# Hybrid decoder layer: a third raw weight tile, a fourth place for split weights, a stock of 72 working tiles, later loads for the per-layer embedding, and queries of heads 0 and 1 built without transfers

## The chip, the cores and the metric

One core of a Trainium2 chip runs the kernel. The metric is device time in microseconds for one execution; the median of three runs is compared. A profile is one further execution, and its times count from its first instruction.

## The reference

One layer over 512 tokens of width 1024, in float32:

```python
h = rmsnorm(x, attn_norm);  proj = h @ w_in
mq, mk, mv, rq, rk, rv, rg = split(proj)          # seven parts of 512 columns
moba = block-sparse attention(mq, mk, mv)          # 8 heads of 64, blocks of 256 keys, ALiBi
ret  = groupnorm(retention(rq, rk, rv)) * silu(rg) # 4 heads of 128, chunks of 256
x = x + concat(moba, ret) @ w_out
h = rmsnorm(x, ffn_norm);  u = causal_dwconv3(h @ w_up)
x = x + (gelu(u) * (h @ w_gate)) @ w_down          # 2816 wide
g = sigmoid(rmsnorm(x, ple_norm) @ w_ple_gate)
x = x + (p @ w_ple) * g                            # per-layer embedding, 256 inputs
out = rmsnorm(x, final_norm)
```

With 512 tokens there are two blocks of 256 keys and three may be chosen, so every allowed block is taken: the attention is plain causal attention with ALiBi.

## The kernel before

**Three products for one.** TensorE multiplies in a reduced float32 format. Each operand is therefore split: a high part, which ScalarE (ACT) rounds, and a low part, the rest, which VectorE (DVE) or GpSimd (POOL) subtracts. `mm3` (L91) issues high x high, high x low and low x high, each with 512 columns.

**Weights.** `fetch` (L127) loads a job of weights, up to 1 MB, from the SP queue into a raw tile `wr`; there are two. `prepare` (L139) splits part after part into pairs of `wh` and `wl` tiles; there are three places for each. A pair holds the 8 slices that one projected tile needs. A place is free again when TensorE has done the last product that reads it. `need` (L158) asks for one part more than the caller uses next. In the attention phase POOL does the subtraction for `wl`, elsewhere DVE does.

**The stock.** All other working tiles, [128, 512] float32 each, come from one pool, `heap`, of `HEAP` = 80 tiles, through `h2k` (L60). A tile goes back when its last reader is done. What needs a tile waits for one.

**Order.** TensorE's order is the program order; a loop at the end (L833) ties each of its instructions to the one before. For the other engines and the queues a planner of the framework writes the order at compile time, with its own costs: an engine takes the earliest instruction of the program that it thinks ready. On the chip each engine then follows its list, and an instruction that waits holds up all behind it.

**The start.** `enter(k)` (L269) transposes block k of x into PSUM (four transposes, `xt`), scales it by the norm's gain `gv` and splits it into h1. The gain comes as rows, `grow`, by a transfer from POOL's queue, and is transposed (L221) ahead of the first `xt`.

**Attention.** `project` (L354) makes one tile of 128 output rows by 512 tokens: 24 matmuls, then DVE scales the PSUM tile into `pt` (L361) and it is split. For `mq` and `mk` the two heads of a tile are brought apart by transfers within the chip's memory: for head e of the pair, one tile holds the high part of its queries in 64 partitions and the low part in the other 64 (L369 to L371), so that one matmul takes both; `mk` gives four tiles, and 8 transfers, in the same manner.

After four retention heads (loop at L609, the last turn of which projects `mk` 0, `mq` 0 and `mk` 1) the MoBA loop (L634) runs i = 0 to 9, two turns for a pair of heads: `moba_scores` (L457) for block i % 2 of pair i // 2, in two steps; `moba_values` of two turns earlier; `moba_turn` (transposes of the probabilities) of the turn before. Between these stand fillers: the other projections `mq` 1 to `mq` 3 in i = 0 to 4, `out_first` (products with the second half of w_out) from i = 1, `ple_product` from i = 5, whose first one needs `ple_weights(0, 0)`, `ple_weights(0, 1)` and both of `ple_turn`.

`softmax` (L446): DVE adds the ALiBi bias and takes the minimum (L449), ACT takes the exponential (L452), DVE the reciprocal (L454) and the scaling (L455). `moba_bias` (L442) makes a head's bias tile on POOL. `ple_load` (L560) brings 1.5 MB from SP's queue into six tiles of the stock; `ple_weights` (L577) turns one of them into a high (ACT) and a low part (POOL); `ple_turn` (L570) transposes p on TensorE and splits it.

After this come the convolutional FFN (two halves of 12 and 10 tiles of 128) and the gate of the embedding with the final norm.

Of the kernel before, what the change touches and what calls it, by code (L numbers as in the profile page):

```python
# [31 lines left out]
RMS_EPS = 1e-6  # L32
GN_EPS = 1e-5
NEG = -3.0e38
HEAP = 80


V_FFN, V_PLE, V_RET, V_CW, V_CB, V_ROWS = 0, 8, 16, 20, 86, 108
# [3 lines left out]
def hybrid_layer_kernel(ctx, tc, x, p, attn_norm, w_in, ret_norm, w_out, ffn_norm, w_up, w_gate,  # L42
# [13 lines left out]
    def nm(s):  # L56
        n_of[s] = n_of.get(s, 0) + 1
        return f"{s}_{n_of[s]}"
# [5 lines left out]
    def ps(s):  # L64
        return psum.tile([P, T], F32, tag="ps", name=nm(s))
# [4 lines left out]
    def f(a):  # L70
        return a.bitcast(F32)
# [55 lines left out]
    def fetch(upto):  # L127
        while issued[0] < min(upto, len(jobs)):
            load, (nk, cols, _), _ = job = jobs[issued[0]]
            raw = wpool.tile([P, 2048], F32, tag="wr", name=nm("wr"), bufs=2)[:, :nk * cols]  # L130
            raw = raw.rearrange("p (k c) -> p k c", k=nk)
            load(raw)
            job[2] = raw
            issued[0] += 1
# [4 lines left out]
    def prepare(upto):  # L139
        while halved[0] < min(upto, len(parts)):  # L140
            key, j, i, heaped = parts[halved[0]]
            final = halved[0] + 1 == len(parts) or parts[halved[0] + 1][1] != j
            fetch(j + 2 if final else j + 1)
            (nk, cols, per), raw = jobs[j][1:]
            if heaped:
                ready[key] = split(raw[:, i, :], "wg")
            else:
                part = raw[:, :, i * per:(i + 1) * per] if per else raw[:, 2 * i:2 * i + 2, :]
                n, c = part.shape[1:]
                hi, lo = (wpool.tile([P, 1024], F32R, tag=tag, name=nm(tag), bufs=3)[:, :n * c].rearrange(  # L150
                    "p (k c) -> p k c", k=n) for tag in ("wh", "wl"))
                nc.scalar.activation(hi, part, AF.Copy)  # L152
                aside = key[0] in ("mv", "rq", "rk", "rg", "mq", "mk", "out") and key not in (("mv", 0), ("mv", 1))
                (nc.gpsimd if aside else nc.vector).tensor_tensor(lo, part, f(hi), op=ALU.subtract)  # L154
                ready[key] = (hi, lo)
            halved[0] += 1
# [35 lines left out]
    make_identity(nc, ident)  # L192
    xn, vraw = [], []
    grow = const.tile([ND, P], F32, name="grow")
    nc.gpsimd.dma_start(grow, attn_norm[0].rearrange("(r c) -> r c", c=P))
    for k in range(ND):
        t = h2k("xn")
        nc.sync.dma_start(t.rearrange("p (t c) -> p t c", t=NT),
# [18 lines left out]
    nc.sync.dma_start(vrow[V_CW:V_CB, :], conv_w[0].rearrange("j (r c) -> (j r) c", c=P))  # L217
    nc.sync.dma_start(vrow[V_CB:V_ROWS, :], conv_b[0].rearrange("(r c) -> r c", c=P))
    fetch(2)
    gv_ps = ps("gv")  # L220
    nc.tensor.transpose(gv_ps[:, :ND], grow, ident[:ND, :ND])  # L221
    gv = const.tile([P, ND], F32, name="gv")
# [44 lines left out]
    ss = const.tile([P, ND, NT], F32, name="ss")  # L267

    def enter(k):  # L269
        tp = ps("xt")  # L270
        for t in range(NT):
            nc.tensor.transpose(tp[:, t * P:(t + 1) * P], xn[k][:, t * P:(t + 1) * P], ident)
        wh = hi_of(vraw[k], "rvw")
        g = gv[:, k:k + 1]
        hi = hi_of(tp, "h1", scale=g)
        r = h2k("xT")
        nc.scalar.activation(r, tp, AF.Copy)
        xT.append(r)
        wl, lo = h2k("rvwl", F32R), h2k("h1l", F32R)
        nc.vector.tensor_tensor(wl, vraw[k], f(wh), op=ALU.subtract)  # L280
        nc.vector.scalar_tensor_tensor(lo, tp, g, f(hi), op0=ALU.mult, op1=ALU.subtract)
        h1.append((hi, lo))
        return wh, wl
# [70 lines left out]
    def project(name, i):  # L354

        w = need((name, i))
        acc = ps("pj")
        for k in range(ND):
            mm3(acc, (w[0][:, k, :], w[1][:, k, :]), h1[k], k == 0, k == ND - 1)
        t = h2k("pt")  # L360
        nc.vector.scalar_tensor_tensor(t, acc, DH ** -0.5 if name == "mq" else 1.0, r1b, op0=ALU.mult, op1=ALU.mult)  # L361
        if name == "rg":
            sil[i] = h2k("sil")
            nc.scalar.activation(sil[i], t, AF.Silu)
        elif name == "mq":

            both = split(t, "mq")
            two = [h2k("mq2", F32R) for _ in range(2)]
            for e in range(2):  # L369
                for part, half in zip(both, HALF):  # L370
                    nc.sync.dma_start(f(two[e][half]), f(part[HALF[e]]))  # L371
            qs[name, i] = two
        elif name == "mk":

            both = split(t, "mk")
            two = [[h2k("mk2", F32R) for _ in range(2)] for _ in range(2)]
            for part, tiles in zip(both, two):
                for e in range(2):
                    for half in HALF:
                        nc.sync.dma_start(f(tiles[e][half]), f(part[HALF[e]]))  # L380
            qs[name, i] = two
        else:
            qs[name, i] = split(t, name)
# [225 lines left out]
    for h in range(HR):  # L609
# [7 lines left out]
        project(*tiles[3 * h + 1])  # L617
        ret_sums(h)
        project(*tiles[3 * h + 2])
    for h in range(2):  # L620
        moba_bias(h)
    ple_load()

    big = [lambda n=n, h=h: project(n, h) for n, h in feature_tiles[15:]]
    mid = [lambda dt=dt: out_first(dt) for dt in range(ND)]
# [8 lines left out]
    for i in range(HM + 2):  # L634
# [11 lines left out]
        for e in range(2):  # L646
            if 1 <= i <= HM:
                moba_turn((i - 1) // 2, (i - 1) % 2, e)
            for go in fills[3 * i + 1 + e]:
                go()  # L650
        if 1 <= i < 5:
            ple_weights((i - 1) // 2, (i - 1) % 2)
        if i in (2, 3):
            ple_turn(i - 2)
    out_accs[2] = out_two(2, range(3))
    for dt in range(0, 4, 2):
        out_two(dt, [3], out_accs[dt])
# [216 lines left out]
```

## Time and profile before

| what | value |
|---|---|
| runs of before, us | 702.09, 702.34, 704.38; median 702.34 |
| profiled execution, us | 704.48 |
| its span, first to last instruction, us | 702.60 |
| mean granted clock of TensorE | 0.995 of full speed |
| busy: PE, DVE, ACT, POOL, us | 685.4, 433.5, 282.7, 125.4 |
| moved, mean rate | 71.91 MB, 102 GB/s |

The span leaves out what lies around the instructions (1.88 us in the profiled execution). PE's busy time is a union of overlapping matmuls, so that its complement is what TensorE stood still.

### The profile page before, as it was taken

To read this page: it belongs to the slowest core of one execution; us is meant where nothing else is said; L and a number is where in the kernel's file an instruction comes from. 1 tells how busy PE (TensorE), PEld (TensorE's weight loads), DVE (VectorE), ACT (ScalarE), POOL (GpSimd) and SP (SyncE) were. 2 spreads that over 40 slices of the span, in tenths; PEclk is the share of its full clock that TensorE was granted. 3 is DMA by queue.
4 is the path that set the end of the run, shared out by engine and by line. 5 is a ranking of instruction groups with operands and counts; after the bars stand their busy time and mean duration, and the time that the engine had idled before them with its cause. 6 is when DMAs were issued, how large, how long until landed. Compare 5 with 4: busy or idle time off the path is not lost.

```text
span 702.6 us, 8467 instructions
## 1 busy us (share of the span) xinstructions
PE 685.4 (98%) x3200; PEld 569.5 (81%) x3200; DVE 433.5 (62%) x784; ACT 282.7 (40%) x459; POOL 125.4 (18%) x100
## 2 busy tenths in 40 slices
PE   9999999998899999999999999999999999999995
PEld 6888888886777888888888888888888888888884
DVE  5675677764577875876556653224565565466497
ACT  5534543333565773553334331122343343354311
POOL 6135242325355211000000000000000000000145
PEclk9999999999999999999999999999999999999999
DMA  8335224338554201233233122233332321345003
GB/s 265 116 103 150 61 76 115 81 91 216 144 169 125 68 2 60 63 118 119 81 100 119 47 88 90 94 121 110 109 115 66 119 67 48 133 137 185 1 1 119
DMA packets 73726, 71.91 MB, mean 102 GB/s; under 512 B 2530, under 2 KB 62806, under 8 KB 73686
## 3 DMA queue, kind: packets, MB, share of 16 engines
q1 hardware_dynamic: 73510, 71.11, 33.4%
q8 instruction: 25, 0.41, 0.2%
q10 hardware_dynamic: 144, 0.26, 0.1%
q14 instruction: 15, 0.12, 0.0%
q0 software_dynamic: 32, 0.00, 0.0%
HBM read 62.97 MB, written 2.10 MB: 93 GB/s over the span
## 4 chain that ended last, share of the span: by engine, by line
PE 89%; DVE 6%; ACT 2%; DMA 2%; issue 1%; POOL 0%; SPq 0%; DVEq 0%; ACTq 0%
PE gate L93 6%; PE gate L95 6%; PE dn L95 6%; PE up L95 6%; PE up L93 6%; PE dn L93 6%; PE gate L94 6%; PE dn L94 6%; PE up L94 6%; PE pj L93 5%; PE pj L94 5%; PE pj L95 4%; PE ou L93 2%; PE ou L94 2%; PE ou L95 2%
## 5 line engine op out<-in xcount | busy, mean ns | idle before, releaser
L152 ACT ACTIVATE wh<-wr 128x1024 fp32r<-128x1024 f32 (+2 forms) x108 | 105.3, 979 | 214.9 <-PE dn L94 66.4
L154 DVE TENSOR_TENSOR wl<-wr,wh 128x1024 fp32r<-128x1024 f32 (+2 forms) x78 | 84.6, 1085 | 44.7 <-ACT wh L152 44.6
L154 POOL TENSOR_TENSOR wl<-wr,wh 128x1024 fp32r<-128x1024 f32 x30 | 73.0, 2432 | 153.9 <-ACT wh L152 152.9
L93 PE MATMUL gate<-h2h,wh 128*128 128x512 f32 x176 | 68.7, 390 | 0.0
L95 PE MATMUL gate<-h2h,wl 128*128 128x512 f32 x176 | 68.5, 389 | 0.0
L94 PE MATMUL gate<-h2l,wh 128*128 128x512 f32 x176 | 68.5, 389 | 0.0
L93 PE MATMUL up<-h2h,wh 128*128 128x512 f32 x176 | 68.5, 389 | 0.0
L94 PE MATMUL up<-h2l,wh 128*128 128x512 f32 x176 | 68.5, 389 | 0.0
L95 PE MATMUL up<-h2h,wl 128*128 128x512 f32 x176 | 68.5, 389 | 0.0
L93 PE MATMUL dn<-ach,wh 128*128 128x512 f32 x176 | 68.5, 389 | 0.0
L94 PE MATMUL dn<-acl,wh 128*128 128x512 f32 x176 | 68.5, 389 | 0.0
L95 PE MATMUL dn<-ach,wl 128*128 128x512 f32 x176 | 68.5, 389 | 0.0
L93 PE MATMUL pj<-h1h,wh 128*128 128x512 f32 x160 | 64.1, 401 | 1.2 <-DVE corner L504 1.1
L95 PE MATMUL pj<-h1h,wl 128*128 128x512 f32 x160 | 63.1, 394 | 0.0
L94 PE MATMUL pj<-h1l,wh 128*128 128x512 f32 x160 | 62.9, 393 | 0.0
L700 POOL MEMSET u<- 128x2 f32 x22 | 2.3, 102 | 290.6 <-DVE c L707 290.6
L711 DVE TENSOR_TENSOR ga<-gate,r2b 128x512 f32<-128x512 f32 x22 | 15.2, 691 | 41.4 <-PE gate L95 41.4
L701 DVE TENSOR_TENSOR u<-up,r2b 128x512 f32<-128x512 f32 x22 | 15.1, 692 | 39.3 <-PE up L95 39.3
L94 PEld LDWEIGHTS dn<-acl,wh 128*128 128x128 f32 x176 | 33.0, 188 | 6.9
L95 PEld LDWEIGHTS gate<-h2h,wl 128*128 128x128 f32 x176 | 33.0, 188 | 6.9
L94 PEld LDWEIGHTS up<-h2l,wh 128*128 128x128 f32 x176 | 33.0, 188 | 6.9
L94 PEld LDWEIGHTS gate<-h2l,wh 128*128 128x128 f32 x176 | 33.0, 188 | 6.9
(233 smaller groups left out, 1415.8 us busy)
## 6 DMA issues: line engine op xcount, KB each, us to landing
wr<-in_w_up_dram SPq DMA_DIRECT2D x11, 1024.0 KB, 5.4
wr<-in_w_gate_dram SPq DMA_DIRECT2D x11, 1024.0 KB, 5.4
wr<-in_w_in_dram SPq DMA_DIRECT2D x20, 512.0 KB, 3.9
wr<-in_w_down_dram SPq DMA_DIRECT2D x8, 768.0 KB, 4.2
wr<-in_w_down_dram SPq DMA_DIRECT2D x8, 640.0 KB, 4.1
wr<-in_w_ple_gate_dram SPq DMA_DIRECT2D x4, 1024.0 KB, 5.1
wr<-in_w_out_dram SPq DMA_DIRECT2D x3, 1024.0 KB, 5.2
xn<-in_x_dram SPq DMA_DIRECT2D x8, 256.0 KB, 5.9
```

The costliest lines, as they stand in the source:

```text
L93: nc.tensor.matmul(acc, a[0], b[0], start=first, stop=False)
L94: nc.tensor.matmul(acc, a[0], b[1], start=False, stop=False)
L95: nc.tensor.matmul(acc, a[1], b[0], start=False, stop=last)
L152: nc.scalar.activation(hi, part, AF.Copy)
L154: (nc.gpsimd if aside else nc.vector).tensor_tensor(lo, part, f(hi), op=ALU.subtract)
L700: nc.gpsimd.memset(u[:, 0:2], 0.0)
L701: nc.vector.tensor_tensor(u[:, 2:], up, r2b, op=ALU.mult)
L711: nc.vector.tensor_tensor(ga, gate, r2b, op=ALU.mult)
```

## The change

Six edits, in the order of the diff: the stock goes from 80 tiles (of 2 KB in each partition) to 72, which gives 16 KB. A third raw tile takes 8 KB, and a fourth place for `wh` and `wl` takes 4 KB each. `grow` is loaded from ACT's queue in place of POOL's, and the first four transposes `xt` stand ahead of that of `gv`. For pair 0 ACT rounds each head's half of the queries straight into the half of the tile where the high part stands, and DVE writes the rest into the other half: two ACT and two DVE instructions on 64 partitions, in place of one and one on 128 and four transfers. The bias of heads 0 and 1 is made in turn 1 of the retention loop. `ple_load` goes from ahead of the MoBA loop to the end of turn 1, `ple_weights` from turns 1 to 4 to turns 3 to 6, `ple_turn` from turns 2 and 3 to turns 3 and 4.

```diff
-HEAP = 80
+HEAP = 72
@@ fetch
-            raw = wpool.tile([P, 2048], F32, tag="wr", name=nm("wr"), bufs=2)[:, :nk * cols]
+            raw = wpool.tile([P, 2048], F32, tag="wr", name=nm("wr"), bufs=3)[:, :nk * cols]
@@ prepare
-                hi, lo = (wpool.tile([P, 1024], F32R, tag=tag, name=nm(tag), bufs=3)[:, :n * c].rearrange(
+                hi, lo = (wpool.tile([P, 1024], F32R, tag=tag, name=nm(tag), bufs=4)[:, :n * c].rearrange(
@@ start
-    nc.gpsimd.dma_start(grow, attn_norm[0].rearrange("(r c) -> r c", c=P))
+    nc.scalar.dma_start(grow, attn_norm[0].rearrange("(r c) -> r c", c=P))
...
+    def turned(k):
+        tp = ps("xt")
+        for t in range(NT):
+            nc.tensor.transpose(tp[:, t * P:(t + 1) * P], xn[k][:, t * P:(t + 1) * P], ident)
+        return tp
+
+    turned_first = turned(0)
     gv_ps = ps("gv")
@@ enter
-        tp = ps("xt")
-        for t in range(NT):
-            nc.tensor.transpose(tp[:, t * P:(t + 1) * P], xn[k][:, t * P:(t + 1) * P], ident)
+        tp = turned(k) if k else turned_first
@@ project, name == "mq"
-            both = split(t, "mq")
             two = [h2k("mq2", F32R) for _ in range(2)]
+            if i == 0:
+                for e in range(2):
+                    nc.scalar.activation(two[e][HALF[e]], t[HALF[e]], AF.Copy)
+                    nc.vector.tensor_tensor(two[e][HALF[1 - e]], t[HALF[e]], f(two[e][HALF[e]]), op=ALU.subtract)
+            both = split(t, "mq") if i else ()
@@ retention loop, then MoBA loop
-    for h in range(2):
-        moba_bias(h)
-    ple_load()
+        if h == 1:
+            for e in range(2):
+                moba_bias(e)
...
-        if 1 <= i < 5:
-            ple_weights((i - 1) // 2, (i - 1) % 2)
-        if i in (2, 3):
-            ple_turn(i - 2)
+        if i == 1:
+            ple_load()
+        if 3 <= i < 7:
+            ple_weights((i - 3) // 2, (i - 3) % 2)
+        if i in (3, 4):
+            ple_turn(i - 3)
```

## Rows read from the trace of the kernel before

**Rows 1.** Windows: length, busy us (count) of five engines, clock, DMA share, GB/s

```profile
150.00:175.00 25.00, 22.15 (x101) 18.11 (x100) 11.17 (x31) 8.26 (x13) 11.99 (x6) 0.93 0.71 190
175.00:200.00 25.00, 22.43 (x115) 18.19 (x114) 17.24 (x52) 13.20 (x33) 13.46 (x7) 1.00 0.67 172
200.00:225.00 25.00, 24.44 (x135) 20.85 (x134) 18.27 (x52) 15.77 (x36) 11.21 (x7) 1.00 0.37 103
...
300.00:400.00 100.00, 100.00 (x444) 82.80 (x444) 62.13 (x81) 40.48 (x50) 1.00 (x10) 1.00 0.32 99
...
650.00:702.60 52.60, 43.92 (x235) 37.16 (x234) 36.86 (x93) 10.67 (x17) 20.09 (x13) 0.97 0.11 41
```

**Rows 2.** Waits of PE: line, released by; us in total, times, longest

```profile
PE ms L470 <- DMA mq<-mql: 2.7, 1, 2.7
...
PE ms L470 <- DVE mkl L82: 1.2, 1, 1.2
PE pj L93 <- DVE corner L504: 1.1, 2, 0.8
PE ou L93 <- DVE ml L449: 0.7, 2, 0.4
PE pw L93 <- DVE corner L504: 0.7, 1, 0.7
```

**Rows 3.** Timeline of PE, 158 to 167: start, duration, what, idle before and releaser

```profile
161.86 0.39 PE L470 MATMUL ms<-mk,mq 128*128 128x256 f32 x1 [2.68 <-DMA mq<-mql]
...
163.33 0.63 PE L95 MATMUL pj<-h1h,wl 128*128 128x512 f32 x1
...
166.74 0.40 PE L94 MATMUL pj<-h1l,wh 128*128 128x512 f32 x1
```

**Rows 4.** Timeline of DVE, 153 to 173

```profile
153.81 2.40 DVE L233 TENSOR_SCALAR rrs<-rrv 128x4 int32<-128x4 int32 x1
...
156.93 0.68 DVE L361 SCALAR_TENSOR_TENSOR pt<-pj,r1b 128x512 f32<-128x512 f32 x1
...
158.31 0.69 DVE L82 TENSOR_TENSOR mql<-pt,mqh 128x512 fp32r<-128x512 f32 x1
...
161.16 1.92 DVE L82 TENSOR_TENSOR mkl<-pt,mkh 128x512 fp32r<-128x512 f32 x1 [0.70 <-ACT mkh L75]
...
172.86 0.16 DVE L454 RECIPROCAL mi<-mt 128x1 f32<-128x1 f32 x1 [8.09 <-ACT me L452]
```

**Rows 5.** Timeline of ACT, 157 to 190

```profile
157.64 0.63 ACT L75 ACTIVATE mqh<-pt 128x512 fp32r<-128x512 f32 x1 [3.41 <-DVE pt L361]
...
169.96 1.06 ACT L152 ACTIVATE wh<-wr 128x1024 fp32r<-128x1024 f32 x1 [8.84 <-PE pj L94]
...
189.16 1.06 ACT L152 ACTIVATE wh<-wr 128x1024 fp32r<-128x1024 f32 x1 [4.47 <-issue]
```

**Rows 6.** Timeline of POOL, 153 to 231

```profile
153.79 2.40 POOL L154 TENSOR_TENSOR wl<-wr,wh 128x1024 fp32r<-128x1024 f32 x1 [5.33 <-ACT wh L152]
160.18 2.36 POOL L154 TENSOR_TENSOR wl<-wr,wh 128x1024 fp32r<-128x1024 f32 x1 [3.99 <-ACT wh L152]
...
229.67 1.29 POOL L581 TENSOR_TENSOR wpl<-wpr,wph 128x512 fp32r<-128x512 f32 x1 [3.09 <-ACT wph L75]
```

**Rows 7.** Timeline of SP's queue, 166 to 169: issues

```profile
166.45 1.98 SPq L564 DMA_DIRECT2D wpr<-in_w_ple_dram  x4
```

**Rows 8.** Chain that ended last, in order of time: start, us, what

```profile
177.45 5.76 DMA mq<-mql
```

**Rows 9.** Timeline of PE, 227 to 229

```profile
228.04 0.40 PE L93 MATMUL pw<-wph,pTh 128*128 128x512 f32 x1
```

**Rows 10.** Timeline of PE and its weight loads, 4 to 8

```profile
4.59 0.24 PE L221 MATMUL gv<-ident,grow 8*128 8x8 f32 x1 [0.19 <-POOL sq L287]
4.76 2.21 PE L272 MATMUL xt<-ident,xn 128*128 128x128 f32 x8
...
7.92 0.29 PEld L95 LDWEIGHTS rv<-rvwh,h1l 128*128 128x128 f32 x1 [0.77 <-DVE h1l L281]
```

## The prediction

> **What bounds the kernel now.** I read the windows first. TensorE (PE) is busy 685.4 of 702.60 us, and from 250 to 650 us it never stands: 444 matmuls in 100 us, 0.225 us apart, are its own pace [rows 1]. Nothing in this change takes a matmul away, so only what PE stands still, or runs slowly, can be won. It stands 17.2 us in all. In 650 to 702.60 it is 8.7 us, nearly all of it after its last matmul, where the last tiles are normed and written; no edit touches that. At the start it is 1.7 us. The rest, 6.7 us, lies in 150 to 250, the MoBA stage: 2.85 and 2.57 us in its first two quarters, then about 0.6 in each of the others [rows 1].
>
> The waits of PE name these: 2.7 us until the last transfer of queries 0 has landed, 1.2 us in the same place for pair 1 (put down to DVE, but it is again the transfer, below), and 2.5 us in five waits for DVE to empty a PSUM tile (1.1, 0.7 and 0.7) [rows 2]. The timeline adds a cost that is no wait: after the 2.68 us the matmuls run 0.43 us apart from 163.33 to 166.74, where 8 take 3.41 us in place of 8 x 0.225 = 1.8. The granted clock of the quarter is 0.93 [rows 1, 3]: 1.6 us are lost to the lower level. The two pairs of ACT and DVE rows show why DVE is late. An ACT instruction that splits a weight part waits 8.84 us for PE to free a place, and the first exponential stands behind it; DVE waits 8.09 us for that exponential. The same happens at 189.16, with 4.47 us [rows 4, 5].
>
> **The change, part by part.** *Queries of heads 0 and 1.* Now `pt` ends at 157.61, ACT rounds until 158.27, DVE subtracts until 159.00, the four transfers follow and PE starts at 161.86, 2.68 us after it ran out of work at 159.18 [rows 3 to 5]. After: ACT rounds head 0's half (at most the 0.63 of the full tile) until 158.27, DVE writes its rest (at most 0.69) until 159.00; head 1's pair follows on ACT until 158.9 and on DVE until 159.7. The trace shows no subtraction that writes into other partitions than it reads; for its cost I take that of the same shape on 128, 0.69, which also is the upper end, and nothing for the lower, since the later head matters only from 159.4, when head 0's two matmuls are over. PE then waits about 0.3 to 0.5 us for head 1. Gain 2.7 - 0.5 = 2.2 us (0.5 to 2.7). A stop of 1.2 us did not lower the clock in 175 to 200 [rows 1, 2], so the 1.6 us return too. The bias made in the retention loop costs POOL the same two instructions earlier, where DVE and PE wait for none of them, and takes POOL out of the way to the first minimum.
>
> *Pair 1.* Its last transfer is issued at 177.45 and takes 5.76 us, behind 1.5 MB of `ple_load`, issued from 166.45 on, and a weight load [rows 7, 8]. Its `pt` itself is late, since DVE is held by the exponential. Both go: the load moves behind turn 1, and the exponential no longer stands behind the weight split, since with a fourth place that split waits for the end of the projection before, 159.0 in place of 169.96. Gain 1.2 us (0 to 1.2).
>
> *Fourth place, third raw tile.* A raw tile more lets a load start a job earlier; in the stretches where PE is full that is worth nothing, and its cover is PE's own 0.225 us pace. In the MoBA stage the fourth place moves 13.3 us of blocked ACT time (8.84 and 4.47) off the softmax [rows 5]. Of the 2.5 us that PE waits for DVE I take half, 1.3 us (0 to 2.5): DVE is the nearest thing to a second bound there, 18.27 us of 25 [rows 1], and part of its lateness is its own.
>
> *Start.* The four transposes `xt` now run at 4.76, behind that of `gv`, which waits for `grow` [rows 10]; in the new order they need block 0 of x alone, and `gv` follows. What this can shorten is the 0.77 us that the weight load at 7.92 stands for the low part of block 0 [rows 10]. The other four transposes of that row wait for the next block of x and don't move, so that PE gets there no earlier. Gain 0.3 us (0 to 0.8). The load on ACT's queue costs ACT an issue while ACT has nothing to do.
>
> *What may be given back.* `ple_weights(0, 1)` moves to turn 4, the place of the present `ple_weights(1, 1)`, whose POOL part ends at 229.67 + 1.29 = 230.96. The first filler that needs it does so at 228.04 [rows 6, 9]. Were engines as late as now, PE would wait 2.9 us; with DVE and ACT less behind I take 0.7 us (0 to 2.9). SP's queue issues the six `ple` loads ahead of turn 2's, and whatever waits there for a tile of the stock waits with them: the transfers of `mk` 2 and `mq` 2, which PE reads in turn 4 only.
>
> *Stock of 72.* I counted, in the order of the program, the tiles whose last reader is still to come. Before, the count is 78 in turn 1, 80 in turn 2 and at most 88 in turn 3, where `mk` 3 is split, against 80. Of these 6, 7 to 10 and 10 belong to the embedding; with its loads later they are 0, 6 and 6, so that the change needs 72, 78 and 84, against 72. The overdraft is 0, 6 and 12 where it was 0, 0 and 8. So some tiles of turns 2 and 3 are handed out late; with eight PSUM tiles between PE and DVE I count nothing for it in the likeliest case, and the rival below prices it.
>
> The sum against the profiled execution: 2.2 + 1.6 + 1.2 + 1.3 + 0.3 - 0.7 = 5.9 us, so its 704.48 would be 698.6. The median of the runs is 702.34, 2.1 below the profiled one; I set the forecast against it: **696.4 us**.
>
> **Rivals.** *The new subtraction is held by POOL.* A POOL split of 2.40 us begins at 153.79, and a four-column DVE instruction beside it takes 2.40 us; the one of 160.18 stretches DVE's `mkl` from 0.69 to 1.92 [rows 4, 6]. If the fourth place moves such a split onto 158.3 to 159.7, head 0's rest ends up to 2.4 us late, PE stops as long as now, and the clock falls as now: 2.2 + 1.6 are lost, 700.2 us. The Trainium skill (SBUF — State Buffer, section Who interferes with whom) has the rule: a VectorE instruction with two inputs in SBUF and a GpSimd instruction that reads SBUF exclude each other for the whole instruction, and the one issued first wins; the two rows agree with it, and by it the two new subtractions, both with two such inputs, are exposed. Against it: POOL is idle from 156.19 to 160.18, and its splits follow the ends of PE's projections, which don't move.
>
> *The weight split still stands ahead of the exponential.* With four places ACT's next split waits for the end of the next projection, and the planner may again list it first. Then DVE's waits stay and pair 1 is late in `pt`, though not in transfers: 2.2 + 1.6 + 0.3 - 0.7 = 3.4, 698.9 us. For it: both blocked splits follow that pattern. Against it: the bias is ready earlier, and so is the exponential.
>
> *What PE wins, it waits for later.* DVE is busy 17.24 of 25 and 18.27 of 25 us in 175 to 225 [rows 1]. If its chain sets the stage's end, PE arrives earlier at the same wait, and about 701.5 us are left. Against it: DVE itself stands 8.09 us in one piece.
>
> *The stock starves (slower).* Place: turn 3, where 84 tiles are asked of 72. If what is held back is the destination of a minimum, its two PSUM tiles stay full, the softmax of block 1 starts only when `moba_values` frees four tiles, and PE reaches the transposes of turn 4 before it. The nearest row for a softmax held back is DVE's 8.09 us [rows 4]; with the clock's 1.6 that is 9.7 us against 6.6 won without it, 705 us. It decides from 6.6 us of standing. For it: the overdraft grows by half. Against it: with 8 too many, before, PE waited only 0.3 us in that turn, the shorter of the two waits for `corner` [rows 2].
>
> **How the numbers follow.** Likeliest 0.56, its own range 693.5 to 699; POOL's hold 0.08; the split still first 0.13; waits later 0.10; starved stock 0.13. With every gain at its upper end (2.7 + 1.6 + 1.2 + 2.5 + 0.8 = 8.8) the time is 693.5. The range 693.4 to 702.4 leaves out the starved stock and a little below. Within 0.3% (2.1 us) a measurement of this kernel can't tell a change from none. Faster: the likeliest, the split, and half of POOL's hold with some of the waits: 0.75. Same: 0.12. Slower: 0.13.
>
> **What would show it.** In the changed profile the first `ms` should follow the projection of `mk` 1 within 0.5 us and no matmul after it be 0.43 apart; ACT's exponentials of pair 0 should come at 160 to 163, not 171; `ms` of pair 1 should wait for nothing; `rv` at 7.92 should move up; the first `pw` shows in its wait whether the late `ple_weights` is in time; 250 to 650 should stay full. Wrong would be a gap of PE of several us between 190 and 225, above all one that ends with a DVE instruction that had waited for a tile, or matmuls at half pace after it.

## The result: 707.23 us, slower by half a per cent

The changed kernel takes 707.23 us (median of 10 runs, 703.65 to 709.44) against 703.11 us for the kernel before in runs beside it (702.09 to 704.84): a ratio of 1.0051, 95% interval 1.0034 to 1.0067. The forecast was 696.4 us with a range up to 702.4. A second set of 9 runs gave 707.01 against 702.91 us, 1.0055 (1.0037 to 1.0074).

The profiled execution took 705.4 us, one of the shorter ones (span 703.5, clock 0.991), and that of the kernel before, 704.48 us, was one of the longer, so that the two traces show less of the loss than the medians have. The windows of the changed kernel, which answer to [rows 1]:

```profile
0.00:25.00 25.00, 21.67 (x96) 17.53 (x97) 12.80 (x21) 12.28 (x21) 10.41 (x17) 0.93 0.92 284
...
150.00:175.00 25.00, 24.54 (x120) 20.41 (x119) 15.99 (x43) 12.27 (x22) 11.52 (x6) 1.00 0.52 137
175.00:200.00 25.00, 21.45 (x109) 17.64 (x108) 14.25 (x42) 12.23 (x28) 9.90 (x6) 1.00 0.77 223
200.00:225.00 25.00, 21.74 (x118) 18.38 (x119) 20.77 (x53) 14.82 (x36) 10.45 (x6) 0.96 0.48 125
225.00:250.00 25.00, 24.65 (x132) 20.83 (x130) 18.14 (x55) 16.58 (x39) 8.34 (x5) 0.98 0.07 23
```

In 150 to 175 PE now stands 0.46 us where it stood 2.85, at the full clock where it had 0.93. In 175 to 225 it stands 6.81 us where it stood 3.13. The first quarter brought what was forecast, the two behind it took it back. PE's waits, to be held against [rows 2]:

```profile
PE ou L93 <- DVE corner L513: 2.3, 1, 2.3
PE xt L223 <- DMA xn<-in_x_dram: 1.9, 1, 1.9
PE ou L93 <- DVE ml L458: 1.7, 1, 1.7
PE mo L522 <- DVE mpl L513: 1.5, 1, 1.5
...
PE pw L94 <- POOL wpl L590: 0.9, 1, 0.9
...
PE ms L479 <- DVE mq L376: 0.5, 1, 0.5
```

And the places of these waits in the timelines of the same execution, PE first, then ACT, DVE and POOL (start, duration, what, idle before and releaser):

```profile
159.77 0.36 PE L479 MATMUL ms<-mk,mq 128*128 128x256 f32 x1 [0.46 <-DVE mq L376]
...
222.62 0.70 PE L93 MATMUL ou<-mxh,wh 128*128 128x512 f32 x1 [2.29 <-DVE corner L513]
223.12 0.63 PE L94 MATMUL ou<-mxl,wh 128*128 128x512 f32 x1
...
250.50 0.50 PE L94 MATMUL pw<-wpl,pTh 128*128 128x512 f32 x1 [0.86 <-POOL wpl L590]
...
165.57 1.06 ACT L152 ACTIVATE wh<-wr 128x1024 fp32r<-128x1024 f32 x1 [1.76 <-PE pj L94]
...
183.82 1.06 ACT L152 ACTIVATE wh<-wr 128x1024 fp32r<-128x1024 f32 x1 [3.80 <-issue]
...
195.88 0.38 ACT L530 ACTIVATE mr<-mo 64x256 f32<-64x256 f32 x1 [3.21 <-DMA mq<-mqh]
...
158.07 0.69 DVE L376 TENSOR_TENSOR mq<-pt,mq 64x512 fp32r<-64x512 f32 x1
...
185.81 1.78 DVE L464 TENSOR_SCALAR me<-me,mi 128x512 f32<-128x512 f32 x1
...
196.29 0.42 DVE L531 TENSOR_TENSOR mt<-mo,mr 64x256 f32<-64x256 f32 x1 [3.02 <-ACT mr L530]
...
199.49 0.69 DVE L513 TENSOR_TENSOR mpl<-mp,mph 128x512 fp32r<-128x512 f32 x1 [0.90 <-ACT mph L512]
...
219.59 2.51 DVE L464 TENSOR_SCALAR me<-me,mi 128x256 f32<-128x256 f32 x1
...
184.96 2.36 POOL L154 TENSOR_TENSOR wl<-wr,wh 128x1024 fp32r<-128x1024 f32 x1 [8.74 <-ACT wh L152]
...
219.61 2.35 POOL L154 TENSOR_TENSOR wl<-wr,wh 128x1024 fp32r<-128x1024 f32 x1 [0.53 <-ACT wh L152]
```

The first scores come at 158.81 (161.86 before), those of pair 1 at 177.74 (182.71), so that PE is 5.0 us ahead. Then it loses this step by step. The row at 183.82 shows the weight split ahead of the exponential once more; POOL's part of that split holds DVE's scaling (185.81, 1.78 us), and PE waits 1.7 us for a minimum. At 195.88 ACT, about to empty the result of `moba_values` into `mr`, waits 3.21 us for a transfer of queries. `mr` doesn't read what that transfer brings; I take it that `mr` needs a tile of the stock, and that the one that comes back next is the source of the transfer (the experiments below bear this out). DVE's `mt` and `mpl` come after it, and PE waits 1.5 us for the latter. At 222.62 it waits 2.29 us for the corner tile, which is late because DVE's scaling ahead of it takes 2.51 us beside the POOL split of 219.61; behind that wait the matmuls run 0.43 us apart: the lower clock. Of these three waits only the second is one for the stock. The transposes that follow the last wait come at 253.91 us, 253.42 before: the lead is gone.

### The profile page after: what moved, and what is told of

Same layout as the page of the kernel before. It is cut to its first block, busy times and chain, and to the rows that moved or that the text cites. A ratio compares the mean times of both kernels' runs of the same rounds, so it can differ in the third digit from the quotient of the medians.

```text
span 703.5 us, 8469 instructions
## 1 busy us (share of the span) xinstructions
PE 682.8 (97%) x3200; PEld 569.4 (81%) x3200; DVE 433.3 (62%) x785; ACT 284.5 (40%) x460; POOL 125.8 (18%) x99
## 4 chain that ended last, share of the span: by engine, by line
PE 87%; DVE 5%; DMA 4%; ACT 2%; issue 1%; POOL 1%; SPq 0%; DVEq 0%; ACTq 0%
PE gate L93 6%; PE dn L95 6%; PE up L93 6%; PE dn L93 6%; PE gate L95 6%; PE gate L94 6%; PE up L94 6%; PE up L95 6%; PE dn L94 6%; PE pj L93 4%; PE pj L94 4%; PE pj L95 4%; PE ou L93 2%; PE ou L94 2%; PE ou L95 2%; DMA mq<-mqh 2%
## 5 line engine op out<-in xcount | busy, mean ns | idle before, releaser
L95 PEld LDWEIGHTS up<-h2h,wl 128*128 128x128 f32 x176 | 33.0, 188 | 6.9
L95 PEld LDWEIGHTS dn<-ach,wl 128*128 128x128 f32 x176 | 33.0, 188 | 6.9
```

The lines of the kernel that those rows point to most:

```text
L95: nc.tensor.matmul(acc, a[1], b[0], start=False, stop=last)
```

## Experiments

All times are medians of 5 to 12 runs, taken in five rounds; a ratio is to the kernel before on the same chip, with its 95% interval. "Restored" is the changed kernel with 2 raw tiles, 3 places and the stock of 80, all other edits kept.

### What the memory trade costs

The whole trade undone:

```diff
-HEAP = 72
+HEAP = 80
...
-            raw = wpool.tile([P, 2048], F32, tag="wr", name=nm("wr"), bufs=3)[:, :nk * cols]
+            raw = wpool.tile([P, 2048], F32, tag="wr", name=nm("wr"), bufs=2)[:, :nk * cols]
...
-                hi, lo = (wpool.tile([P, 1024], F32R, tag=tag, name=nm(tag), bufs=4)[:, :n * c].rearrange(
+                hi, lo = (wpool.tile([P, 1024], F32R, tag=tag, name=nm(tag), bufs=3)[:, :n * c].rearrange(
```

> The changed kernel with both memory edits undone: two raw tiles, three places, a stock of 80; everything else as changed. If the smaller stock gives the gain back (theory S), no engine waits for a tile of the stock in 185 to 200 us any more, PE keeps the 5 us it has won by its first products of pair 1, and the time is 697 to 700 us. If it is the order of weight splits and the subtractions that POOL and DVE hold each other up with (theory P), the 1.7 and 2.3 us waits of PE stay in some form and the time stays at 703 to 707. If the late embedding weights cost most (theory L), the wait of the first pw products stays and the time is above 703.

Measured: 702.28 us, 0.9992 (0.9979 to 1.0005). The same in parts. Only the raw tile undone, which leaves room for a stock of 76:

```diff
-HEAP = 72
+HEAP = 76
...
-            raw = wpool.tile([P, 2048], F32, tag="wr", name=nm("wr"), bufs=3)[:, :nk * cols]
+            raw = wpool.tile([P, 2048], F32, tag="wr", name=nm("wr"), bufs=2)[:, :nk * cols]
```

> The changed kernel with two raw tiles and a stock of 76, four places kept. Theory S: in turns 2 and 3, 78 and 84 tiles are asked of 76, so about half of the give-back goes: 700 to 704 us. Theory P: the places are the same, so the waits for DVE stay: 705 to 708.

Only the fourth place undone, again with 76:

```diff
-HEAP = 72
+HEAP = 76
...
-                hi, lo = (wpool.tile([P, 1024], F32R, tag=tag, name=nm(tag), bufs=4)[:, :n * c].rearrange(
+                hi, lo = (wpool.tile([P, 1024], F32R, tag=tag, name=nm(tag), bufs=3)[:, :n * c].rearrange(
```

> The changed kernel with 3 raw tiles, 3 places and a stock of 76 (the run with 2 raw tiles, 4 places and 76 gave 701.8 us). Theory stock: 76 is nearly enough in turns 2 and 3 (78 and 84 asked), so 702 to 704 us, ratio 0.998 to 1.001. Theory raw tile: the third raw tile lets weight loads go ahead of the queries' transfers on SP's queue, so 705 to 708 us with PE or ACT waiting for those transfers, ratio 1.003 to 1.007, although the stock is 76.

Raw tile and place both undone, as in the first diff, but with `HEAP = 72` kept:

> The changed kernel with 2 raw tiles and 3 places as before, but the stock still 72: of the memory trade only its price is left. Theory stock: the price is all there is, so 707 us or a little more (706 to 709), ratio 1.005 to 1.008, and the profile shows ACT or DVE waiting 3 us or more for a DMA of the queries' halves in 175 to 225 us (a tile of the stock handed out late) and PE waiting for the low part of the probabilities. Theory raw tile and places: those two disturb the order of the loads and splits and the stock costs nothing, so 702.3 us as with the stock of 80, ratio 0.999.

Measured: 701.80 us, 0.9983 (0.9969 to 0.9996); 703.13 us, 0.9996 (0.9983 to 1.001); and 710.4 us, 1.0094 (1.0078 to 1.011). Between the restored kernel and the one with 72 alone only the stock differs: it costs 7 us by the ratios, 8 by the medians. The raw tile and the place together give 3 of them back, so that the whole trade costs 4 to 5 us (707.23 against 702.28; 1.0051 against 0.9992). In the kernel with 72 alone the chain is the same as in the changed one, only longer. From its timelines of ACT and PE:

```profile
197.20 0.38 ACT L530 ACTIVATE mr<-mo 64x256 f32<-64x256 f32 x1 [5.57 <-DMA mq<-mqh]
...
198.96 0.50 PE L479 MATMUL ms<-mk,mq 128*128 128x512 f32 x1 [2.37 <-DVE mt L531]
...
201.56 0.58 PE L522 MATMUL mo<-corner,mv 128*128 128x256 f32 x1 [1.87 <-DVE mpl L513]
...
205.63 0.78 PE L93 MATMUL ou<-mxh,wh 128*128 128x512 f32 x1
```

With the stock of 80 the same `mr` waits for nothing, and neither in this run nor in the kernel before does ACT or DVE wait a full microsecond for a transfer of queries or keys from 160 to 240 us:

```profile
191.65 0.38 ACT L530 ACTIVATE mr<-mo 64x256 f32<-64x256 f32 x1
```

With 76 there is such a wait, but for a later taker of a tile and with less behind it: in the run with four places ACT waits 3.74 us, PE 1.0 us.

```profile
198.81 0.60 ACT L512 ACTIVATE mph<-mp 128x512 fp32r<-128x512 f32 x1 [3.74 <-DMA mq<-mql]
```

The changed kernel run once more, for a second profile:

> The changed kernel once more, for a second profile and for times on the same chip as the three below. Either theory: 707 us, ratio 1.005 to 1.007. Its profile should show the waits of the first one (PE 1.5 us for the low part of the transposed probabilities, 1.7 for a minimum, 2.3 for the corner tile) and, if it falls on a longer execution, either more of the same waits or a lower granted clock behind them; a new wait in another stage would speak against the theory that the stock of tiles is the loss.

It showed the same waits, 1.9 us in place of 1.5, then 1.7 and 2.3. In it PE comes to the first scores 1.9 us earlier (156.92 against 158.81), and yet it is only 0.1 us ahead at the values' products of turn 4 (212.92 against 213.06) and at its last matmul: this lead too is lost in the MoBA stage.

The traces of the changed and the restored kernel show where the difference arises. At 184 us the changed one is 0.4 us ahead. The wait for a minimum (1.7 us, none in the restored one) and that for `mpl` (1.5 us, none) put it 2.5 us behind. Around the corner tile it loses 1.1 us more, though it waits less there, 2.29 against 3.07 us, since its matmuls then run at the lower clock. The 3.75 us that it is behind then stay to the end.

### Where the demand comes from

`mr` and `mt` get tiles of their own, in the kernel with 72 alone:

```diff
-        rest, t = h2k("mr"), h2k("mt")
+        rest, t = (wpool.tile([P, 256], F32, tag=s, name=nm(s), bufs=4) for s in ("mr", "mt"))
```

> The run with 2 raw tiles, 3 places and a stock of 72 (710.4 us), with one edit: the two tiles into which moba_values moves its result (mr and mt, 1 KB each) no longer come from the stock but from four small tiles each of their own. Theory, what the stock makes late is mr: ACT's wait of 5.6 us for the transfers of queries before the first mr goes, and with it PE's 2.4 and 1.9 us behind it and the half-rate matmuls after them; the time falls from 710.4 to 704 to 706 us, ratio 1.001 to 1.004. Rival, the stock is short of tiles for everything in these turns: the next taker (the high and low parts of the transposed probabilities, or the result of a softmax) waits for the same transfers instead, and the time stays at 708 to 710 us, ratio 1.007 to 1.010.

Measured: 707.17 us, 1.006 (1.0048 to 1.0072): between the two. `mr` no longer waits; the next that takes a tile does, on ACT:

```profile
198.84 0.42 ACT L532 ACTIVATE mxh<-mt 128x256 fp32r<-128x256 f32 x1 [5.99 <-DMA mq<-mqh]
```

So it is no matter of one buffer: in turn 3 there are too few tiles for whoever comes. The prediction's count says that six of them hold the embedding. Its load goes behind turn 3, in the kernel with 72 alone and in the changed kernel itself:

```diff
-        if i == 1:
+        if i == 3:
             ple_load()
-        if 3 <= i < 7:
-            ple_weights((i - 3) // 2, (i - 3) % 2)
-        if i in (3, 4):
-            ple_turn(i - 3)
+        if i == 4:
+            for k in range(2):
+                ple_weights(0, k)
+                ple_turn(k)
+        if i in (5, 6):
+            ple_weights(1, i - 5)
```

> The run with 2 raw tiles, 3 places and a stock of 72 (710.4 us), with the embedding's load at the end of turn 3 in place of turn 1 and its splits and transposes in turns 4 to 6, so that its six tiles are not held in turns 2 and 3. Theory, it is the demand of turn 3 over the stock that costs: by the count of the prediction turn 3 then asks 78 of 72 in place of 84, ACT's 5.6 us before the first mr shrinks to 3 us or less and PE's waits for mt and mpl with it; what is new is PE's wait for the embedding's late low part, 1 to 3 us. Time 704 to 707.5 us, ratio 1.001 to 1.006. Rival, the tiles that are short are those of the queries' split in transit and the embedding has no part in it: mr waits as long as before, the embedding's wait comes on top, 710 to 713 us, ratio 1.010 to 1.014.

> The change itself (3 raw tiles, 4 places, stock of 72; 707.2 us) with the embedding's load at the end of turn 3 and its splits and transposes in turns 4 to 6. Theory demand: the waits for mr and for the low part of the probabilities shrink, 703 to 705.5 us, ratio 1.000 to 1.003. Rival, the embedding has no part: 707 to 710 us, ratio 1.005 to 1.010.

Measured: 702.8 us, 1.0003 (0.9985 to 1.002), and 702.44 us, 0.9984 (0.9969 to 0.9998): all of the loss is gone, below what was expected. In the first of the two `mr` stands at 191.58 with no wait, as with the stock of 80; in the second, which keeps the four places, the waits for a minimum and for `mpl` are gone too, and the 3.1 us for a corner tile stay. But the edit moves tiles, 1.5 MB of traffic and the splits and transposes of turn 3 together. Two runs were to part the first two, with the six tiles outside the stock (and the load again at the end of turn 1):

```diff
-                t = ple_in["w", c, k] = h2k("wpr")
+                t = ple_in["w", c, k] = wpool.tile([P, T], F32, tag="ple", name=nm("wpr"), bufs=6)
...
-            t = ple_in["p", j] = h2k("pn")
+            t = ple_in["p", j] = wpool.tile([P, T], F32, tag="ple", name=nm("pn"), bufs=6)
```

> The run with 2 raw tiles, 3 places and a stock of 72 (710.4 us), with the embedding's load where the change has it, at the end of turn 1, but into six tiles of its own, outside the stock. The late load (702.8 us) took the six tiles and 1.5 MB of transfers out of turns 2 and 3 together; this run takes the tiles alone. Theory tiles: 702 to 704 us, ratio 0.999 to 1.002, with mr waiting for no transfer. Rival traffic: the embedding's transfers, ahead of those of the queries on SP's queue, keep the queries' tiles from coming back, so 708 to 711 us, ratio 1.007 to 1.011, with ACT's wait of some 5 us for them as before.

Measured: 702.85 us, 0.9994 (0.9977 to 1.001). The time is that of the theory. The splits stay in turns 3 to 6 here, so that their place isn't what costs. But tiles and traffic are not parted: the view of the tile shows the load issued long before, since it no longer waits for a tile.

```profile
L573 SPq DMA_DIRECT2D wpr<-in_w_ple_dram x4: 346/438/448, 15.9 to 17.3; - x4
```

So the stock was cut as well, until turn 3 was as short as in the kernel with 72 alone, now without the traffic:

```diff
-HEAP = 72
+HEAP = 66
```

> The run before it (the embedding's load in six tiles of its own, 702.85 us; its traffic had moved to 16 us after the start) with the stock cut from 72 to 66. Turn 3 then asks 78 of 66, 12 too many, as the stock of 72 with the embedding's tiles in it (84 of 72, 710.4 us), but with none of the embedding's traffic in turns 2 and 3. Theory tiles: ACT again waits 4 us or more for the queries' transfers before mr or mxh in 188 to 200 us, 707 to 711 us, ratio 1.006 to 1.012. Rival traffic: without it the transfers give their tiles back in time, no such wait over 2 us, 702 to 704.5 us, ratio 0.999 to 1.003.

Measured: 707.57 us, 1.0062 (1.0042 to 1.0081). The time is that of the tiles' theory, but most of it is lost earlier than the theory had it. By the same count the stock of 66 is also 6 tiles short in turn 1, where the kernel with 72 alone is not short at all. The rows of DVE and ACT:

```profile
176.25 0.76 DVE L82 TENSOR_TENSOR mxl<-rt,mxh 128x512 fp32r<-128x512 f32 x1 [3.59 <-DMA mq<-mqh]
...
197.94 0.38 ACT L530 ACTIVATE mr<-mo 64x256 f32<-64x256 f32 x1 [2.34 <-DMA mq<-mqh]
```

Against the run before it PE is 0.5 us behind at the last scores of turn 1 (172.35 against 171.84) and 4.7 us at those of turn 2 (187.33 against 182.58). The wait for `mr` in turn 3, 2.34 us, adds 1.5 us, and 6.1 us are left at the end. So a shortage costs its 4 to 5 us without the embedding's traffic. What 12 too many in turn 3 cost by themselves, and how much the traffic lengthened the 5.57 us there, these runs don't show.

### Where the forecast gain went

Restored, the kernel should have shown the gains without the stock's loss and without the fourth place's 1.3 us: 4.6 us. It shows 1.05 by the medians (702.28 against 703.33) and 0.6 by the ratio, which its interval can't tell from nothing. The edits one by one. The start alone, in the kernel before:

```diff
-    nc.gpsimd.dma_start(grow, attn_norm[0].rearrange("(r c) -> r c", c=P))
+    nc.scalar.dma_start(grow, attn_norm[0].rearrange("(r c) -> r c", c=P))
...
+    turned_first = turned(0)
     gv_ps = ps("gv")
...
+        tp = turned(k) if k else turned_first
```

> The kernel before with the start's edits alone: the gain's rows from ACT's queue and the first four transposes ahead of those of the gain. My prediction said 0.3 us less, 702.8. If the second block of x lands later because a second hardware queue is busy beside SP's (theory T), PE stands for it at about 5 to 7 us and the time is 703.5 to 704.5.

Measured: 702.63 us, 0.999 (0.9977 to 1.0002). The queries without transfers and the earlier bias alone, in the kernel before:

```diff
+            if i == 0:
+                for e in range(2):
+                    nc.scalar.activation(two[e][HALF[e]], t[HALF[e]], AF.Copy)
+                    nc.vector.tensor_tensor(two[e][HALF[1 - e]], t[HALF[e]], f(two[e][HALF[e]]), op=ALU.subtract)
+            both = split(t, "mq") if i else ()
...
         project(*tiles[3 * h + 2])
-    for h in range(2):
-        moba_bias(h)
+        if h == 1:
+            for e in range(2):
+                moba_bias(e)
     ple_load()
```

> The kernel before with the queries of heads 0 and 1 built without transfers, and their bias made in the retention loop; all else as before. By my prediction 3.8 us go at that place and 1 to 2 more at pair 1: 698 to 700 us. If whatever PE wins there is waited for later in the MoBA stage in any case (theory P, or a DVE that is the bound), the first products move up by 3 us and the FFN does not: 702 to 703.5.

Measured: 709.13 us, 1.0086 (1.007 to 1.0103), far from both theories. The first scores come early (159.63), and pair 1 pays for it. Its timelines of PE, DVE and SP's queue:

```profile
185.66 0.55 PE L474 MATMUL ms<-mk,mq 128*128 128x256 f32 x1 [7.69 <-DMA mq<-mql]
...
186.65 0.63 PE L93 MATMUL pj<-h1h,wh 128*128 128x512 f32 x1
...
160.72 2.39 DVE L244 TENSOR_TENSOR rrt<-rry 128x4 f32<-128x4 f32 x1
...
163.42 0.69 DVE L361 SCALAR_TENSOR_TENSOR pt<-pj,r1b 128x512 f32<-128x512 f32 x1
...
164.80 2.38 SPq L384 DMA_DIRECT2D mk<-mkh  x4
...
170.11 1.96 SPq L568 DMA_DIRECT2D wpr<-in_w_ple_dram  x4
...
174.48 3.75 SPq L115 DMA_DIRECT2D wr<-in_w_out_dram  x1
...
178.34 1.43 SPq L375 DMA_DIRECT2D mq<-mqh  x2
```

With `ple_load` at its old place six loads and the next weights stand in the queue ahead of the transfers of pair 1. They stood there before too; new is that the queue is late. A four-column DVE instruction takes 2.39 us beside the POOL split that begins at 160.70, ahead of `pt` of `mk` 1, which starts at 163.42 in place of 159.78. The transfers of `mk` 1 go out at 164.80 in place of 161.15, and all behind them with them. So PE is at pair 1 sooner, its queries land later (it starts at 185.66, 182.71 before), it waits 7.69 us, and it runs its next matmuls at the lower clock. In the changed kernel the hold is there as well (160.09, 2.25 us), but the load no longer stands in between, and pair 1 waits 0.59 us. From this I take it that the late load makes the edit possible; a run with these two edits alone was not made. The other way round, the restored kernel with the transfers of pair 0 put back:

```diff
-            if i == 0:
...
-            both = split(t, "mq") if i else ()
+            both = split(t, "mq")
```

> The changed kernel with 2 raw tiles, 3 places and the stock of 80 (702.3 us), but with the queries of heads 0 and 1 again split whole and moved by four transfers; the rest of the change stays. Theory, the queries' edit wins its 2.7 us and the clock's 1.6 and they last: 705.5 to 706.5 us, ratio 1.003 to 1.005, with PE's wait of about 2.7 us for the transfer of mq and half-rate matmuls behind it. Rival, what PE wins there it waits for later, for DVE in 175 to 225 us: the wait for the transfer comes back, a later one goes, and the time is 702 to 703.5 us, ratio 0.998 to 1.001.

Measured: 703.38 us, 1.0004 (0.9994 to 1.0014). PE's waits in it:

```profile
PE ms L475 <- DMA mq<-mql: 3.2, 2, 2.7
...
PE ms L475 <- DVE corner L509: 1.3, 1, 1.3
```

The 2.7 us are back. The restored kernel's 3.1 us for a corner tile are gone, and 1.3 us for another stand at 207.88. By the ratios the edit is worth 0.0012 of the time, 0.8 us, which the two intervals can't tell from nothing; together they allow some 2 us, not the 3.8 us at its own place. The traces are kinder to it. PE's last matmul, in the restored kernel and in this one:

```profile
690.40 0.28 PE L95 MATMUL pg<-wgh,h3l 128*128 128x256 f32 x1
...
693.31 0.28 PE L95 MATMUL pg<-wgh,h3l 128*128 128x256 f32 x1
```

The restored kernel leads by 4.15 us at the last scores of pair 0 (173.20 against 177.35) and still by 2.9 at the end. But its profiled execution (701.16 us) was one of its shortest, and that of the other (704.0) was longer than its median. So part of what PE wins there it waits for later; how much is open. The rows of the restored kernel at its longest wait, from DVE, POOL and PE:

```profile
216.90 2.50 DVE L464 TENSOR_SCALAR me<-me,mi 128x256 f32<-128x256 f32 x1
...
219.51 0.35 DVE L464 TENSOR_SCALAR me<-me,mi 128x256 f32<-128x256 f32 x1
219.78 0.55 DVE L513 TENSOR_TENSOR corner<-mp,corner 128x384 fp32r<-128x384 f32 x1
...
216.91 2.35 POOL L154 TENSOR_TENSOR wl<-wr,wh 128x1024 fp32r<-128x1024 f32 x1 [0.47 <-ACT wh L152]
...
220.38 0.50 PE L93 MATMUL ou<-mxh,wh 128*128 128x512 f32 x1 [3.07 <-DVE corner L513]
```

POOL's split of output weights holds DVE's scaling for 2.50 us, 0.35 without it, and the corner tile is late. So this split goes to DVE in the restored kernel:

```diff
-                aside = key[0] in ("mv", "rq", "rk", "rg", "mq", "mk", "out") and key not in (("mv", 0), ("mv", 1))
+                aside = key[0] in ("mv", "rq", "rk", "rg", "mq", "mk") and key not in (("mv", 0), ("mv", 1))
```

> The changed kernel with 2 raw tiles, 3 places and the stock of 80 (702.3 us), and one edit more: the low parts of the output weights are made by DVE and no longer by POOL. Theory port: the 2.50 us of a DVE tensor_scalar beside POOL's 2.35 us split (alone it takes 0.35) is what puts the corner tile late, so PE's wait of 3.1 us before an output product goes, and with it the half-rate matmuls where they follow: 699 to 700.5 us, ratio 0.994 to 0.997. Rival, DVE is full: DVE takes about 1 us for each of these splits in the same stage, where it is busy 18 of 25 us, so the wait moves and the time stays at 702 to 704 us, ratio 0.999 to 1.002.

Measured: 703.69 us, 1.0008 (0.9993 to 1.0022). The wait for the corner tile is gone, and another stands at a place where the restored kernel has none:

```profile
179.75 0.42 PE L479 MATMUL ms<-mk,mq 128*128 128x256 f32 x1 [3.29 <-DMA mk<-mkh]
```

Next the embedding's splits one turn earlier, alone and with that edit:

```diff
-        if 3 <= i < 7:
-            ple_weights((i - 3) // 2, (i - 3) % 2)
+        if 2 <= i < 6:
+            ple_weights((i - 2) // 2, (i - 2) % 2)
```

> The changed kernel with 2 raw tiles, 3 places and the stock of 80 (702.3 us), with the four splits of the embedding's weights one turn earlier (turns 2 to 5; the load stays at the end of turn 1). Theory: PE's wait of 0.9 us for a low part of these weights goes and nothing else moves, so 701.4 us, ratio 0.997 to 0.999. Rival: the splits' ACT and POOL parts now stand in the fullest turns, POOL holds DVE's scaling once more, and PE waits longer for the corner tile or a minimum: 702.5 to 704 us, ratio 0.999 to 1.002.

> The changed kernel with 2 raw tiles, 3 places and the stock of 80 (702.3 us), with the low parts of the output weights on DVE (alone: 703.7 us, with a wait of 3.3 us for a transfer of the keys in place of the 3.1 us for the corner tile) and the embedding's weights one turn earlier. Theory, each wait that an edit removes is only replaced by one that the written order of the queues makes: 702 to 704 us, ratio 0.999 to 1.002, with a stop of 2 us or more at a place where the run without the edits has none. Rival, the two edits remove 3.1 and 0.9 us and their side effects don't add up: 699 to 700.5 us, ratio 0.994 to 0.997.

Measured: 701.47 us, 0.9974 (0.9961 to 0.9988), in time as the theory had it, with the 0.9 us for the low part gone (against the restored kernel's 0.9992 the intervals overlap, and two new waits of 0.8 and 0.5 us stand in the trace); and 702.63 us, 0.9998 (0.9984 to 1.0011), where a stop of 3.02 us stands before the scores at 179.43, now put down to a minimum:

```profile
179.43 0.55 PE L479 MATMUL ms<-mk,mq 128*128 128x256 f32 x1 [3.02 <-DVE ml L458]
```

With the output weights on DVE the wait for the corner tile is replaced, both times, by one of 3 us or more in the same 50 us. That is shown; that it would be so for every order of the queues is not, and the earlier split, which replaced its 0.9 us by smaller waits only, is a first exception.

### The version that the runs point to

2 raw tiles, 4 places, a stock of 76, and the splits one turn earlier:

```diff
-HEAP = 72
+HEAP = 76
...
-            raw = wpool.tile([P, 2048], F32, tag="wr", name=nm("wr"), bufs=3)[:, :nk * cols]
+            raw = wpool.tile([P, 2048], F32, tag="wr", name=nm("wr"), bufs=2)[:, :nk * cols]
...
-        if 3 <= i < 7:
-            ple_weights((i - 3) // 2, (i - 3) % 2)
+        if 2 <= i < 6:
+            ple_weights((i - 2) // 2, (i - 2) % 2)
```

> 2 raw tiles, 4 places and a stock of 76 (701.8 us), with the embedding's splits one turn earlier, which took 0.8 us off the run with 3 places and the stock of 80 (701.47 us). Theory, with enough tiles for turn 3 what is left are single waits and this one goes: 701 us, ratio 0.996 to 0.998. Rival, the earlier splits hold tiles in the turns where 76 is just enough: mr waits for a transfer again, 702.5 to 704.5 us, ratio 0.999 to 1.002.

Measured: 700.58 us (697.52 to 702.62), 0.9955 (0.9936 to 0.9973): faster than both kernels. Against the run with the earlier splits in the restored kernel (0.9974) it can't be told apart, so that the place and the 4 tiles less have no gain shown of their own. What PE still waits for in it:

```profile
PE ou L93 <- DVE ml L458: 1.7, 1, 1.7
...
PE mp L510 <- DVE pTl L82: 1.2, 1, 1.2
PE ms L479 <- DVE ml L458: 1.2, 1, 1.2
...
PE mo L522 <- DVE mpl L513: 0.4, 1, 0.4
```

No wait of PE over 1.7 us is left in the stage, and the late low part (`mo`) is down to 0.4 us.

## Why the prediction was wrong

**The step that failed is the stock.** The sentence "with eight PSUM tiles between PE and DVE I count nothing for it in the likeliest case" put at nothing a term that measures 7 to 8 us by itself (710.4 us, 1.0094, against 702.28, 0.9992) and 4 to 5 us with the raw tile and the place beside it. The rival built on the count of tiles, the starved stock at 705 us, came nearest; it got 0.13.

The count was right, but it isn't a price. The forecast held up that 8 tiles too many had cost 0.3 us before, and took half as many more for nearly as cheap. By that same count the runs give, for turn 3: 4 too many (restored) 702.28 us; 6 (72 with the late load) 702.8; 8 (76 with places or raw tile) 701.80 and 703.13; 12 (72 alone) 710.4 (the change itself, also 12, 707.23). These runs differ in more than the count, and none has 9 to 11. Nor does one count cost the same everywhere: 8 too many of 80 held no engine up for a full microsecond before, 8 of 76 held ACT up for 3.74 us but PE for 1.0 only, and in the run with 66 tiles 6 too many in turns 1 and 2 cost PE 4.2 us. The rival also named the wrong tile: not the destination of a minimum was held back, but `mr`, which empties the values' PSUM tile.

**The gains of pair 0 were right at their place, that of pair 1 half.** PE waits 0.46 us in place of 2.7 for the queries of pair 0 (forecast 0.3 to 0.5), and no matmul behind it is at the lower clock. For pair 1 it still waits 0.59 us, 1.2 before; the forecast was that it waits for nothing.

**Their sum was not.** It added gains from the places where they arise and took them to last to the end. The rival "what PE wins, it waits for later", 701.5 us with a chance of 0.10, is near what the restored kernel takes (702.28 us, 0.9992). Queries and clock, 3.8 us in the sum, are worth 0.8 us by the ratios, and 2 at most; the one pair of traces has 2.9. How much of it is waited for later stays open.

**The fourth place did not free ACT.** The forecast had the split ahead of the first exponential wait for the projection before, until 159.0 in place of 169.96. The split that stands there still waits for the end of the projection of `mq` 1, now at 165.57, as its rival said. That the wait there shrank from 8.84 to 1.76 us is not the place's doing: the restored kernel, with three, has 1.62, and 2.97 at the second split, where the changed one has 3.80 (4.47 before). Its rows from ACT:

```profile
166.13 1.06 ACT L152 ACTIVATE wh<-wr 128x1024 fp32r<-128x1024 f32 x1 [1.62 <-PE pj L94]
...
184.25 1.06 ACT L152 ACTIVATE wh<-wr 128x1024 fp32r<-128x1024 f32 x1 [2.97 <-issue]
```

The first exponential comes at 167.94, 172.34 before; the forecast was 160 to 163. PE's 1.7 us for a minimum stand behind the second split. In the restored kernel POOL holds the same scaling for 1.67 us, but DVE's list has the minimum ahead of it, and PE doesn't wait.

**Small terms.** The late embedding split costs 0.9 us (forecast 0.7), but not at the first `pw`, which waits for nothing: it is the split of turn 6, read at 250.50 in turn 7. The start brought nothing: `rv` begins at 7.27 us, 6.65 before, since the second block of x lands later in the profiled execution (1.86 us of waiting), and the first 25 us have the clock at 0.93. In the second profile `rv` begins at 6.10 and the clock is 1.00, and alone the edit can't be told from no change.

**POOL's hold** fell on another place than its rival said: the new subtractions took 0.69 us each, undisturbed, as their upper bound had it, while a four-column DVE instruction at 160.09 took 2.25 us beside the next POOL split. This made `pt` of `mk` 1 late (162.46, 159.78 before), and with it the queue behind it; the forecast had no term for that.

## What to carry to other kernels

Before trading working tiles for buffers of another kind, count the live tiles turn by turn, and take the count as a sign of where it is short, not of what that costs: an overdraft that cost nothing so far says nothing of one half as large again, or of the same one elsewhere. Ask what holds tiles through the worst turn without being read there; moving that load behind the turn made a stock of 72 as fast as one of 80. And a wait removed early in a stage counts only as far as the later waits of the same stage let it, so test the sum by undoing one edit in the finished kernel, not only by adding it to the old one: the queries' edit costs 6 us alone, and beside the late load it wins 2 us at most.

## What the runs showed of the hardware

The subtraction that reads 64 partitions and writes the 64 others takes 0.69 us for 512 columns, as long as one on 128 partitions in place [rows 4].

A DVE scaling of 128x256, with one tile and a column of factors as inputs, took 2.50 us beside POOL's split, although by the profile it began 0.01 us before it (216.90 and 216.91), and 0.35 us alone; in the changed kernel it took 2.51 us (219.59 and 219.61). The Trainium skill (SBUF — State Buffer, section Who interferes with whom) lists this operation among those that can take the port pair shared with GpSimd, for the whole instruction, and says that the one issued first has it. The length agrees with it; on the order these rows can't decide, since POOL's spans are rough. Of the two rows that the prediction held to agree with the rule for two inputs in SBUF, only that of `mkl` has two; the four-column one is a `TENSOR_SCALAR` like the scaling and reads one tile.

The length of a stop alone doesn't tell whether TensorE's clock falls. In the restored kernel PE stood 3.07 us before 220.38 and ran on at the full clock (0.23 us apart, 1.00 in 200 to 225). In the run with the earlier splits it stood as long at the same wait and ran on at the lower clock (0.93), and so did the changed kernel after 2.29 us (0.43 us apart, 0.96). What made the difference these runs don't show.
